# MLP of an encoder layer: weight sums on VectorE, their stores a step later, first rows and updated rows asked for steps ahead

## The chip, the cores and the metric

The kernel runs on one core of a Trainium2 chip. The metric is the device time of one execution, in microseconds (us). "Before" and "after" name the kernel without and with the change.

## The reference

One encoder layer, sequence 2048, width 1024, all in float32. Only the end of it matters here:

```python
x = x + gt1 * (mixed @ w_o)                       # end of the mixer
h = rmsnorm(x, g_norm2) * (1.0 + sc2) + sh2
x = x + gt2 * (jnp.square(jax.nn.relu(h @ w1)) @ w2)   # w1: 1024 x 4096, w2: 4096 x 1024
```

Ahead of it stand the conditioning vector, the input projection, stick-breaking attention, chunked attention and the output projection `mixed @ w_o`.

## The kernel before

Activations are kept transposed: 128 features on the partitions, 512 tokens along a row, so that there are four token blocks. A float32 product is made of three matmuls (`mm3`): ScalarE casts the operand to its high part, VectorE subtracts to get the low part (`split`), and TensorE multiplies high by high, high by low and low by high. One `operand` is thus a cast on ScalarE and a subtraction on VectorE. Operands lie in a pool of eight buffers (`opp`).

The MLP cuts its matrices into two by two quarters and makes seven products where eight would be the plain way. The operands of these products are sums and differences of quarters: quarters have the names "11", "12", "21", "22", the products the numbers 1 to 7. Product 1 uses quarter "11" itself, 2 uses "12", 4 uses "22", and 5, 6, 3 and 7 use sums that VectorE or GpSimd make (`column_sum`). The order is `OUTER = (1, 5, 6, 3, 7, 2, 4)`. Products share three banks (`HOME`): 1 and 2 the first, 5 and 3 the second, 6, 7 and 4 the third. The third bank is seeded by ScalarE with a copy of product 1 (`ps_s<-ps`); products 5 and 6 are copied out by ScalarE (`cp<-ps`) before 3 and 7 add to their banks.

The work of this last part is a list of steps, in the order in which TensorE runs them:

- `Mixed`: eight steps, one for a row block of the output projection of the last token block; 24 matmuls each. `residual` adds the result to x on VectorE, and the row is stored.
- `First(mb, j, i)`: product i of pair j (16 pairs of w1 chunks, seven products each), for the token pair `mb`, 12 matmuls. It runs for `mb` 1, and after `plain` stages for `mb` 0. A result goes through squared ReLU to the scratch `scr_hid`.
- `Second(mb, i, j)`: product i of the second matrix by hidden rows (`plain`), 16 steps of 12 matmuls. Its operands come as `hw` from `scr_hid` and w2 or `scr_s`.
- `Outer(i, q, k)`: 56 steps of 6 matmuls for one i (`outer`, for i of 7, 2, 3, 4), with a second level of seven products inside. Its operands come as `l` (weights) and `r` (hidden rows).

After the `First` steps of `mb` 1 come `plain(1, 1)`, `plain(1, 6)`, `plain(1, 5)`, then the `First` steps of `mb` 0, then `plain(0, 1)`, `outer(7)`, `plain(0, 6)`, `outer(2)`, `plain(0, 5)`, `outer(3)`, `outer(4)`.

Each engine works through its instructions in the order in which the program traces them. That order is written out by hand: `at(n, job)` puts a job at step n, and `Later.add(ticks, job)` puts one so many step ends later, with the step end of its own step counted. At each step the main loop first prepares operands of later steps as long as eight operand buffers suffice, then loads a mixer row, then makes the operands of the first two `First` steps (at the last `Mixed` step only), then traces the jobs of the step, then the step's own matmuls and what follows on them:

```python
while nxt is not None and ready - used + nxt.tiles <= 8:
    nxt.prepare()
...
for job in jobs.get(n, ()):
    job()
s.run()
...
later.tick()
```

The jobs that matter here:

- `First.load` asks for a pair of w1 chunks (two DMAs into tile `w`); `First.fetch` loads if that hasn't been done and makes the pair's four sums, in tiles `ts` (pool `tp`, seven buffers) and, for product 7, in place. For the first two pairs of `mb` 1 the sums are on GpSimd.
- `second_sums` loads w2 chunks (`w2s`) while `First` of `mb` 1 runs, makes four sums in place on VectorE and stores each to `scr_s` at once. `outer_sums` does the same with `wt` and `scr_t` while `First` of `mb` 0 runs.
- `raw_pair` gives the buffers for `w`, `w2s`, `wt`, `hw` and `l`, in turn from a ring of three and from one spare.
- `plain_loads` asks for the `hw` pairs of a `plain` stage, so many steps ahead of each.
- `load_x` asks for the rows of x (`txo` in pool `tp`, `cxo` in a pool of twelve) that an `outer` stage updates, quarter by quarter: "22" at the products 5 and 7, "12" at 6 and 3, "11" at 2, "21" at 4. `weigh` updates them on VectorE from the bank, and they are stored at the end of the step after.

All of these DMAs are issued by the one sync queue (SP), in the order of the program too: a store that waits for VectorE holds back the loads behind it.

Of the kernel before, what the change touches and what calls it, by code (L numbers as in the profile page):

```python
# [24 lines left out]
KT = D // P  # L25
# [54 lines left out]
def encoder_kernel(ctx, tc, xT, c, g1, g2, w_in, w_rest, gqk, bias, w_o, w1, w2, w_ada, b_ada, out):  # L80
# [1202 lines left out]
    PLAIN = (1, 6, 5)  # L1283
    DOUBLE = (7, 2, 3, 4)
    OUTER = (1, 5, 6, 3, 7, 2, 4)
    HOME = {1: 1, 2: 1, 5: 5, 3: 5, 6: 6, 7: 6, 4: 6}
    HP = NP // 2
    CN = TB // 2
# [5 lines left out]
    if True:  # L1294
# [138 lines left out]
        class Step:  # L1433
            tiles = frees = 1

            def prepare(self):
                pass

# [3 lines left out]
        class First(Step):  # L1442
# [4 lines left out]
            def __init__(self, mb, j, i):  # L1447
                self.mb, self.j, self.i, self.nm = mb, j, i, f"{mb}_{j}_{i}"
                if mb and j == 0 and i in OUTER[:2]:
                    self.tiles = self.frees = 0  # L1450

            def prepare(self, home=None):
                if (home is None) != (self.tiles > 0):
                    return
                d, i = First.pair[self.mb, self.j], self.i
                self.w = operand(d[{1: "11", 2: "12", 4: "22"}.get(i, i)], f"w{self.nm}", dst=home)

            def load(self):
                d, j = First.pair.setdefault((self.mb, self.j), {}), self.j
# [9 lines left out]
            def fetch(self, m=None):  # L1469
                d = self.load()  # L1470
                for n in range(4) if m is None else (m,):
                    pr, a, b, op = ((5, "21", "22", ALU.add), (6, 5, "11", ALU.subtract), (3, "12", 6, ALU.subtract), (7, "11", "21", ALU.subtract))[n]
                    d[pr] = column_sum(pool if self.mb and self.j < 2 else dve, d["21"] if pr == 7 else temp(f"s{self.nm}_{pr}"), d[a], d[b], op)
                return d

            def run(self):
# [70 lines left out]
        def second_sums(j, step):  # L1547

            t = []

            def load():
                t.append(raw_pair([P, 2, 2, TB], F32, f"w2s_{j}"))
                for s in range(2):
                    sp.dma_start(t[0][:, s].rearrange("p r n -> p (r n)"), w2[2 * j + s])

            def out(i, dst, a, b, op):
                tile = {nm: t[0][:, s, r, :] for nm, s, r in (("11", 0, 0), ("21", 0, 1), ("12", 1, 0), ("22", 1, 1))}
                column_sum(dve, tile[dst], tile[a], tile[b], op)
                sp.dma_start(scr_s[i - 1 if i < 7 else 0, j // 2][:, j % 2, :], tile[dst])

            at(step - (6 if j else 0), load)
            sums = ((5, "22", "21", "22", ALU.add), (7, "21", "11", "21", ALU.subtract))
            sums += ((6, "11", "22", "11", ALU.subtract), (3, "12", "12", "11", ALU.subtract))
            for n, x in enumerate(sums):
                at(step + n + (0 if j else 4), lambda x=x: out(*x))

        class Second(Step):

# [100 lines left out]
        def outer_sums(i, m, step):  # L1669

            t = []

            def load():
                t.append(raw_pair([P, 2, 2, TB], F32, f"wt{i}_{m}"))
                for a in range(2):
                    if i in (3, 7):
                        sp.dma_start(t[0][:, a], scr_s[i - 1 if i < 7 else 0, HP // 2 * a + m])
                        continue
                    r, s = {2: (0, 1), 4: (1, 1)}[i]
                    j = HP * a + 2 * m  # L1680
                    for q in range(2):
                        sp.dma_start(t[0][:, a, q, :], w2[2 * (j + q) + s][:, r * TB : (r + 1) * TB])

            def sums(pr, dst, a, b, op):
                v = {nm: t[0][:, h, :, c * CN : (c + 1) * CN] for nm, h, c in (("11", 0, 0), ("12", 1, 0), ("21", 0, 1), ("22", 1, 1))}
                column_sum(dve, v[dst], v[a], v[b], op)
                sp.dma_start(scr_t[i, pr][:, 2 * m : 2 * m + 2, :], v[dst])

            at(step - 6, load)
            todo = ((5, "22", "21", "22", ALU.add), (7, "21", "11", "21", ALU.subtract))  # L1690
            todo += ((6, "11", "22", "11", ALU.subtract), (3, "12", "12", "11", ALU.subtract))
            for n, x in enumerate(todo):
                at(step + n, lambda x=x: sums(*x))
# [89 lines left out]
        def outer(i, plan):  # L1783

            f = len(steps)
            steps.extend(Outer(i, q, k) for q in range(7) for k in range(HP))
            for g in range(HP // 2):
                for pr, (begin, gap) in plan["load"].items():
                    at(begin + gap * g, lambda pr=pr, g=g: half(i, pr, g))
                for pr, (begin, gap) in plan["sum"].items():  # L1790
                    at(begin + gap * g, lambda pr=pr, g=g: half_sum(i, pr, g))
            for q in range(7):
                at(f + HP * q - 12, steps[f + HP * q].load)
            for pr, b in ((5, "22"), (6, "12"), (2, "11"), (4, "21")):
                s = steps[f + HP * OUTER.index(pr)]
                at(f + HP * OUTER.index(pr) + 1, lambda s=s, b=b: s.load_x(b))
            return f

        class Mixed(Step):
# [40 lines left out]
        steps += [Mixed(0, (KT - LEFT + n) % KT, n) for n in range(KT)]  # L1840
        for n in range(KT):
            steps[n].then = lambda n=n: (
                steps[n + LEFT].load() if n + LEFT < KT else steps[KT].fetch() if n + LEFT == KT else None
            )
        for mb in (1, 0):
            begin = len(steps)
# [2 lines left out]
            for j in range(NP):  # L1849
                f = steps[begin + 7 * j]  # L1850
                if mb:
                    second_sums(j, begin + 7 * j + 2)
                else:
                    outer_sums(DOUBLE[j // 4], j % 4, begin + 7 * j + 5)
                    if j < HP:
                        for i, n in ((3, 2), (2, 5), (7, 2), (4, 5)):
                            at(begin + 7 * j + n, lambda i=i, f=f: f.other(i))
                if j > mb:
                    at(begin + max(7 * j - 13, 2 if mb else -6), f.load)
                    for m in range(4):  # L1860
                        at(begin + 7 * j - 9 + (m if j > 1 else 0), lambda f=f, m=m: f.fetch(m))
            if mb:
                for m, n in enumerate((-1, -1, 1, 2)):
                    at(begin + n, lambda m=m, f=steps[begin + 7]: f.fetch(m))
                norm2(1, begin + 18)
                norm2(0, begin + 48)
                for k in range(HK):
# [14 lines left out]
                at(f + m - (leads.pop(0) if leads else 7), steps[f + m].load)  # L1882

        f = plain(0, 1)
        plain_loads(f, [])
        e = len(steps)
        plan = {"load": {1: (f - 5, 1), 5: (f - 1, 1), 3: (f + 4, 2), 2: (f + 18, 2)}}
        plan["sum"] = {6: (f + 9, 2), 7: (f + 13, 2), 4: (f + 44, 2)}
# [50 lines left out]
        ahead = iter(steps[1:])  # L1939
        nxt = next(ahead)  # L1940
        for n, s in enumerate(steps):
            while nxt is not None and ready - used + nxt.tiles <= 8:
                nxt.prepare()
                ready += nxt.tiles
                nxt = next(ahead, None)
            for m in (0, 1) if n == 0 else (n + 1,):
                if m < KT:
                    steps[m].load_row()
            if n == KT - 1:
                firsts = spare.tile([P, 2, 2, TB], F32R, tag="r8", name="opr")  # L1950
                for m in range(2):
                    steps[KT + m].prepare(firsts[:, m])
            for job in jobs.get(n, ()):
                job()
            s.run()
            used += s.frees
            later.tick()
# [42 lines left out]
```

## Time and profile before

| | us |
|---|---|
| median of three runs | 2568.27 |
| lowest and highest | 2566.47, 2568.61 |
| the profiled execution | 2568.92 |
| its span on the page | 2567.2 |
| TensorE busy in the span | 2534.1 |
| VectorE, ScalarE, GpSimd busy | 2012.0, 1496.2, 760.8 |

How to read the lines: a row of the timeline has its start and its length in us, engine, line of the program, operation, what it writes and reads by the tiles' names, the shape, and how many instructions were merged ("x12"). A bracket gives the engine's idle time before it and who ended it. PE is TensorE, DVE VectorE, ACT ScalarE, POOL GpSimd, SPq the sync queue. Nearly all rows have line L42, which is the helper that all go through, so rows are found by tile. A row of a table of stretches gives, after the stretch, its length and the busy us (with instructions) of PE, PE's weight loads, DVE, ACT and POOL, then the granted clock of TensorE, the busy share of the DMA engines, and GB/s. A row of waits gives who waited for whom, the total, how often and the longest.

### The profile page before, as it was taken

Reading aid. Unit: us, or ns where it says so; the run is one execution under the profiler, and the core shown is the slowest. Engines: PE = TensorE matmul, PEld = TensorE weight load, DVE = VectorE, ACT = ScalarE, POOL = GpSimd, SP = SyncE. Lnnn points to the kernel's source line nnn. Section 1 sums busy time; section 2 is a strip of 40 time slices with the busy share of each in tenths; the row PEclk is TensorE's granted clock in tenths of the full one; section 3 lists DMA queues with packets and bytes.
Section 4 is the critical chain, followed back from the end, with each engine's and each line's share of the span. In section 5 each row is a group of like instructions: output and inputs, shape, how many; then the busy total and the mean of one; then the engine's idle time right before and its main releaser. Section 6 shows DMA issues by size and latency. Waiting matters only on the chain.

```text
span 2567.2 us, 39419 instructions
## 1 busy us (share of the span) xinstructions
PE 2534.1 (99%) x12436; PEld 2109.1 (82%) x12436; DVE 2012.0 (78%) x3501; ACT 1496.2 (58%) x2871; POOL 760.8 (30%) x1136
## 2 busy tenths in 40 slices
PE   9999999999999999999999999999999999999999
PEld 7888888888888888887887888888888878788887
DVE  7656767887789878998867777668978657988897
ACT  6333435668866687666755555566555545646565
POOL 4330145776776667777612000000000000000000
PEclk9999999999999999999999999999999999999999
DMA  9879978689877788756786888787899779677872
GB/s 351 332 298 363 342 281 293 213 237 290 277 239 233 238 279 272 248 193 196 224 309 243 286 285 274 260 306 267 275 323 304 273 254 409 246 272 265 291 268 82
DMA packets 293200, 698.92 MB, mean 272 GB/s; under 512 B 31360, under 2 KB 83584, under 8 KB 281856
## 3 DMA queue, kind: packets, MB, share of 16 engines
q1 hardware_dynamic: 291696, 691.69, 78.1%
q10 hardware_dynamic: 1296, 4.72, 0.5%
q8 instruction: 98, 1.61, 0.2%
q14 instruction: 110, 0.90, 0.1%
HBM read 477.66 MB, written 218.63 MB: 271 GB/s over the span
## 4 chain that ended last, share of the span: by engine, by line
PE 86%; DVE 5%; ACT 3%; DMA 2%; issue 2%; POOL 1%; SPq 1%; DVEq 0%; POOLq 0%; ACTq 0%
PE ps L42 29%; PE ps_s L42 14%; PE pt L42 11%; PE acc L42 6%; PE wt L42 6%; PE po L42 4%; PE z L42 4%; PE pf L42 4%; PE pq L42 3%; PE cz L42 2%; DVE p L42 2%; PE pso L42 1%; DVE opr L42 1%; PE ct L42 1%; ACT z L42 1%
## 5 line engine op out<-in xcount | busy, mean ns | idle before, releaser
L42 PE MATMUL ps<-h,opw 128*128 128x512 f32 x1512 | 361.7, 392 | 3.6 <-ACT cp L42 3.6
L42 ACT CAST wth<-wt 128x512 fp32r<-128x512 f32 (+3 forms) x544 | 257.4, 484 | 172.4 <-PE wt L42 162.5
L42 POOL TENSOR_TENSOR b<-p 128x512 f32<-128x512 f32 (+1 forms) x320 | 292.5, 914 | 167.9 <-DVE p L42 91.9
L42 PEld LDWEIGHTS ps<-h,opw 128*128 128x128 f32 x1512 | 285.7, 189 | 63.6 <-ACT cp L42 4.0
L42 DVE TENSOR_TENSOR wtl<-wt,wth 128x512 fp32r<-128x512 f32 (+3 forms) x544 | 291.2, 547 | 59.2 <-ACT wth L42 56.7
L42 PE MATMUL pt<-w,ht 128*128 128x512 f32 x1248 | 288.2, 391 | 0.0
L42 PE MATMUL ps_s<-h,opw 128*128 128x512 f32 x1152 | 278.6, 391 | 3.2 <-ACT ps_s L42 3.2
L42 PEld LDWEIGHTS pt<-w,ht 128*128 128x128 f32 x1248 | 233.0, 188 | 47.7
L42 PE MATMUL ps<-oph,opv 128*128 128x512 f32 x1152 | 263.8, 391 | 2.5 <-DVE txo L42 2.5
L42 DVE TENSOR_TENSOR_SCAN p<-z,p,zero 128x512 f32<-128x512 f32 x192 | 245.7, 1281 | 25.6 <-ACT z L42 18.6
L42 PEld LDWEIGHTS ps_s<-h,opw 128*128 128x128 f32 x1152 | 217.1, 189 | 48.8 <-ACT ps_s L42 3.6
L42 PEld LDWEIGHTS ps<-oph,opv 128*128 128x128 f32 x1152 | 217.2, 189 | 48.4 <-DVE txo L42 3.0
L42 PE MATMUL acc<-wth,v 128*128 128x512 f32 (+3 forms) x544 | 220.5, 409 | 0.0
L42 ACT CAST opr<-r 128x512 fp32r<-128x512 f32 x224 | 139.3, 623 | 107.7 <-PE ps L42 51.1
L42 ACT ACTIVATE z<-z 128x512 f32<-128x512 f32 (+1 forms) x320 | 166.5, 521 | 55.2 <-PE z L42 49.3
L42 PE MATMUL z<-k,q 128*128 128x512 f32 (+3 forms) x640 | 185.6, 372 | 7.7 <-DVE p L42 7.2
L42 PE MATMUL acc<-wtl,v 128*128 128x512 f32 (+3 forms) x544 | 185.4, 347 | 0.0
L42 PE MATMUL ps<-opr,ol 128*128 128x512 f32 x768 | 176.4, 389 | 0.1
L42 DVE TENSOR_TENSOR opr<-r,opr 128x512 fp32r<-128x512 f32 x224 | 151.2, 688 | 27.5 <-ACT opr L42 24.8
L42 PE MATMUL wt<-ident,b 128*128 128x128 f32 x1088 | 171.4, 273 | 1.1 <-DVE cols L42 0.3
L42 PEld LDWEIGHTS wt<-ident,b 128*128 128x128 f32 x1088 | 136.3, 140 | 42.2 <-DVE cols L42 1.8
L42 PEld LDWEIGHTS ps<-opr,ol 128*128 128x128 f32 x768 | 144.0, 188 | 30.5 <-DVE ol L42 0.4
(218 smaller groups left out, 4862.8 us busy)
## 6 DMA issues: line engine op xcount, KB each, us to landing
q<-scr_q SPq DMA_DIRECT2D x128, 256.0 KB, 4.7
w<-in_w_dram SPq DMA_DIRECT2D x64, 512.0 KB, 5.8
r<-scr_hid SPq DMA_DIRECT2D x64, 512.0 KB, 7.5
k<-scr_k SPq DMA_DIRECT2D x240, 128.0 KB, 4.3
v<-scr_v SPq DMA_DIRECT2D x120, 256.0 KB, 3.9
wa<-in_w_ada_dram SPq DMA_DIRECT2D x48, 512.0 KB, 6.4
ow<-scr_wo SPq DMA_DIRECT2D x24, 1024.0 KB, 5.8
hw<-scr_hid SPq DMA_DIRECT2D x48, 512.0 KB, 6.4
```

What stands on the lines that cost most here:

```text
L42: return lambda *x, **y: self.tc.keep_in_program_order(f(*x, **y))
```

## The change

The sums of the first two pairs move from GpSimd to VectorE. The first pair's load stays at `Mixed` step 5, but its sums are traced at the last `Mixed` step between the operands that need them; jobs of that step now come ahead of these operands. The second pair's load and sums move from the last `Mixed` step and the steps after to steps 1 to 4 of the `First` stage, and `ready()` holds back the preparing of an operand whose sum hasn't been traced. `second_sums` and `outer_sums` store each sum at the end of the next step. The first sums of `w2s` come one step earlier. The first `hw` pair of `plain(0, 1)` is asked for nine steps ahead in place of seven. The rows of the quarters "12", "11" and "21" are asked for five steps ahead of their product's first step in place of one step behind it, "22" as before.

```diff
+    OUTER_NAME = {1: "11", 2: "12", 4: "22"}
...
         class Step:
+            def ready(self):
+                return True
...
         class First(Step):
+            def ready(self):
+                return OUTER_NAME.get(self.i, self.i) in First.pair.get((self.mb, self.j), ())
...
             def fetch(self, m=None):
-                    d[pr] = column_sum(pool if self.mb and self.j < 2 else dve, d["21"] if pr == 7 else temp(f"s{self.nm}_{pr}"), d[a], d[b], op)
+                    d[pr] = column_sum(dve, d["21"] if pr == 7 else temp(f"s{self.nm}_{pr}"), d[a], d[b], op)
...
         def second_sums(j, step):
-                sp.dma_start(scr_s[i - 1 if i < 7 else 0, j // 2][:, j % 2, :], tile[dst])
+                later.add(2, lambda: sp.dma_start(scr_s[i - 1 if i < 7 else 0, j // 2][:, j % 2, :], tile[dst]))
...
-                at(step + n + (0 if j else 4), lambda x=x: out(*x))
+                at(step + n + (0 if j else 3), lambda x=x: out(*x))
...
         def outer_sums(i, m, step):
-                sp.dma_start(scr_t[i, pr][:, 2 * m : 2 * m + 2, :], v[dst])
+                later.add(2, lambda: sp.dma_start(scr_t[i, pr][:, 2 * m : 2 * m + 2, :], v[dst]))
...
         def outer(i, plan):
-                at(f + HP * OUTER.index(pr) + 1, lambda s=s, b=b: s.load_x(b))
+                at(f + HP * OUTER.index(pr) + (1 if b == "22" else -5), lambda s=s, b=b: s.load_x(b))
...
-                steps[n + LEFT].load() if n + LEFT < KT else steps[KT].fetch() if n + LEFT == KT else None
+                steps[n + LEFT].load() if n + LEFT < KT else steps[KT].load() if n + LEFT == KT else None
...
+                if j > mb or mb and j:
                     for m in range(4):
-                        at(begin + 7 * j - 9 + (m if j > 1 else 0), lambda f=f, m=m: f.fetch(m))
+                        at(begin + (m + 1 if mb and j == 1 else 7 * j - 9 + (m if j > 1 else 0)), lambda f=f, m=m: f.fetch(m))
             if mb:
-                for m, n in enumerate((-1, -1, 1, 2)):
-                    at(begin + n, lambda m=m, f=steps[begin + 7]: f.fetch(m))
...
         f = plain(0, 1)
-        plain_loads(f, [])
+        plain_loads(f, [9])
...
-            while nxt is not None and ready - used + nxt.tiles <= 8:
+            while nxt is not None and ready - used + nxt.tiles <= 8 and nxt.ready():
...
+            for job in jobs.get(n, ()):
+                job()
             if n == KT - 1:
                 firsts = spare.tile([P, 2, 2, TB], F32R, tag="r8", name="opr")
-                for m in range(2):
-                    steps[KT + m].prepare(firsts[:, m])
-            for job in jobs.get(n, ()):
-                job()
+                steps[KT].prepare(firsts[:, 0])
+                steps[KT].fetch(0)
+                steps[KT + 1].prepare(firsts[:, 1])
+                for m in range(1, 4):
+                    steps[KT].fetch(m)
             s.run()
```

More of the change, by code (lines that the diff above doesn't have):

```diff
@@ L1455, in prepare @@
                 d, i = First.pair[self.mb, self.j], self.i
-                self.w = operand(d[{1: "11", 2: "12", 4: "22"}.get(i, i)], f"w{self.nm}", dst=home)
+                self.w = operand(d[OUTER_NAME.get(i, i)], f"w{self.nm}", dst=home)
             def load(self):
```

## Prediction

> **What bounds the kernel now.** I read the page's first line and its busy shares first, then the list of what TensorE waited for, kept to the MLP (the change touches nothing ahead of it).
>
> ```profile
> span 2567.2 us, 39419 instructions
> ...
> PE 2534.1 (99%) x12436; PEld 2109.1 (82%) x12436; DVE 2012.0 (78%) x3501; ACT 1496.2 (58%) x2871; POOL 760.8 (30%) x1136
> ```
>
> ```profile
> PE ps L42 <- ACT cp L42: 3.6, 1, 3.6
> PE ps_s L42 <- ACT ps_s L42: 3.2, 1, 3.2
> PE ps L42 <- DVE txo L42: 2.5, 1, 2.5
> PE po L42 <- DMA ow<-scr_wo: 1.0, 1, 1.0
> ```
>
> TensorE is busy for 99% of the span and the change removes no matmul. All that an edit of the order can win in the MLP is therefore in three waits of TensorE, of 3.2, 3.6 and 2.5 us (the fourth line lies ahead of the MLP), and in what each wait drags behind it. I looked each up in the timeline.
>
> **First wait, start of the MLP.** TensorE rows of the first pair of w1 chunks:
>
> ```profile
> 1365.46 5.60 PE L42 MATMUL ps<-h,opr 128*128 128x512 f32 x24
> ...
> 1374.24 4.21 PE L42 MATMUL ps_s<-h,opw 128*128 128x512 f32 x12 [3.18 <-ACT ps_s L42]
> ...
> 1384.16 2.88 PE L42 MATMUL ps<-h,opw 128*128 128x512 f32 x12
> ```
>
> The price of a step comes from the chain of waits, at a place without a wait (first row), and the clock from a table of stretches (its third column from the right is the granted clock):
>
> ```profile
> 2121.12 65.28 PE ps L42 x288
> ```
>
> ```profile
> 1365.00:1390.00 25.00, 21.82 (x89) 17.59 (x88) 17.29 (x18) 11.84 (x22) 11.08 (x7) 0.93 0.39 150
> ...
> 2244.00:2260.00 16.00, 14.48 (x57) 11.81 (x58) 12.43 (x18) 4.84 (x9) 0.00 (x0) 0.89 1.03 377
> ```
>
> 65.28 us for 288 matmuls is 0.2267 us each, 2.72 us for a `First` step of 12. From 1365.46 to 1384.16 lie five steps, worth 13.60 us, and they took 18.70: 5.10 us lost, 3.2 of it standing and the rest slow. The row of 12 behind the wait lasts 4.21 us, and a mean clock of 0.93 over 25 us is 3.5 us at half rate. A wait thus costs itself and about 1.7 us more.
>
> Why it stood:
>
> ```profile
> 1360.21 0.84 SPq L42 DMA_DIRECT2D w<-in_w_dram  x2
> ...
> 1362.67 1.80 POOL L42 TENSOR_TENSOR ts<-w 128x512 f32<-128x512 f32 x1 [59.04 <-ACT h L42]
> 1363.24 0.74 DVE L42 SCALAR_TENSOR_TENSOR cxr<-pso,mod,cxr 128x512 f32<-128x512 f32 x1
> ...
> 1364.01 3.73 SPq L42 DMA_DIRECT2D scr_x<-cxr  x2
> ...
> 1369.61 2.18 ACT L42 CAST opw<-w 128x512 fp32r<-128x512 f32 x4 [1.08 <-POOL w L42]
> ...
> 1372.98 0.62 ACT L42 CAST opw<-ts 128x512 fp32r<-128x512 f32 x1 [0.67 <-POOL ts L42]
> 1373.62 0.57 ACT L42 COPY ps_s<-ps 128x512 f32<-128x512 f32 x1
> ```
>
> The third step needs the bank seeded by the copy at 1373.62. ScalarE works in order, and that copy stands behind eight casts, the last of which wait for GpSimd's sums of the *second* pair.
>
> **Second wait, end of the last `First` stage.** Here are the sync queue, ScalarE and TensorE:
>
> ```profile
> 2085.45 1.25 SPq L42 DMA_DIRECT2D scr_hid<-cz  x1
> ...
> 2091.99 4.76 SPq L42 DMA_DIRECT2D scr_t<-wt  x2
> ...
> 2099.23 0.47 SPq L42 DMA_DIRECT2D hw<-scr_hid  x1
> ...
> 2100.69 2.88 PE L42 MATMUL ps_s<-h,opw 128*128 128x512 f32 x12
> ...
> 2105.40 0.62 ACT L42 CAST oph<-hw 128x512 fp32r<-128x512 f32 x1 [6.11 <-DMA hw<-scr_hid]
> ...
> 2106.55 0.58 ACT L42 COPY cp<-ps 128x512 f32<-128x512 f32 x1
> ...
> 2107.18 5.49 PE L42 MATMUL ps<-h,opw 128*128 128x512 f32 x12 [3.61 <-ACT cp L42]
> ...
> 2118.24 2.88 PE L42 MATMUL ps_s<-h,opw 128*128 128x512 f32 x12
> ```
>
> Between 2100.69 and 2118.24 are four steps, 10.88 us, which took 17.55: 6.67 us lost. The sync queue issued nothing from 2086.7 to 2092, then two stores of `wt` that waited for VectorE's sums, and so the first `hw` load left at 2099.23 only. Its cast waited 6.11 us for it, and the copy that frees the bank stood behind the cast.
>
> **Third wait, end of the first `outer`.**
>
> ```profile
> 2222.26 2.29 SPq L42 DMA_DIRECT2D scr_x<-cxo  x4
> ...
> 2231.35 2.72 DVE L42 SCALAR_TENSOR_TENSOR cxo<-ps,mod,cxo 128x512 f32<-128x512 f32 x4
> ...
> 2234.49 4.61 SPq L42 DMA_DIRECT2D txo<-scr_x  x4
> ...
> 2241.46 1.52 PE L42 MATMUL ps<-oph,opv 128*128 128x512 f32 x6
> ...
> 2245.52 19.83 PE L42 MATMUL ps<-oph,opv 128*128 128x512 f32 x79 [2.54 <-DVE txo L42]
> ```
>
> ```profile
> 2311.36 10.88 PE ps_s L42 x48
> ```
>
> From 2241.46 to 2311.36 are again 288 matmuls (16 `Second` steps of 12 and 16 `Outer` steps of 6), which cost 69.90 instead of 65.28 us: 4.62 lost. The rows `txo` of quarter "21" were asked for at 2234.49, behind stores that waited for VectorE's `cxo`, and came after the bank was done.
>
> In all 5.10 + 6.67 + 4.62 = 16.4 us.
>
> The Trainium skill, "TensorE: Matmul & The Clock Gate", section "What's actually happening", has the clock halved after about one idle window of 3.4 us, in windows that run free of the kernel. By that rule only the 3.61 us wait would drag a slow stretch, and the three would be worth 3.2 + 6.7 + 2.5 = 12.4 us. This trace differs: 2.54 us of standing was enough (0.89 over 16 us is 3.5 us at half rate). The measurement decides.
>
> **The change part by part.**
>
> ```profile
> L42 DVE TENSOR_TENSOR ts<-w x30: 681/685/694, 1385.6 to 2072.9; 128x512 f32<-128x512 f32 x30
> ...
> DMA to landing us min/median/max: 4.2/5.7/7.4
> ```
>
> ```profile
> w2s<-in_w_dram SPq DMA_DIRECT2D x2, 512.0 KB, 3.6
> ```
>
> (The first is the durations of the sums, the second the landing times of all w1 chunks, the third that of two loads issued at 1371.13 into an idle queue.)
>
> *Sums on VectorE, in the new order.* Eight sums go from GpSimd to VectorE at 0.69 us. VectorE is in order: last row but one of the mixer till 1363.98, low part of "11" 1364.67, sum 5 1365.36, then ScalarE's cast (0.62) 1365.98, low part of 5 1366.67, sums 6, 3 and 7 at 1367.36, 1368.05, 1368.74, the last mixer row 1369.5. TensorE's second step begins at 1368.18, so its operand is in time. ScalarE casts 6, 3, 7, "12", "22" behind the sums, till 1370.6, and the copy ends at 1371.2. `ready()` keeps the second pair's casts behind it. Due is 1365.46 + 5.44 = 1370.90, so 0.3 us late.
>
> The second pair's load moves from 1360.21 to step 9, on the sync queue behind the store of the last mixer row, about 1369.8. Its first sum stands on VectorE in front of the first pair's combinations, and two of its casts on ScalarE in front of the copy of product 6, which TensorE needs for the first pair's fifth step at 1376.3. Landing 3.6 to 5.7 us after the second issue (1370.2): 1373.8 to 1375.9; sum, cast and copy add 1.9, so 1375.7 to 1377.8: a new wait of 0 to 1.5 us. The slowest landing of the trace, 7.4, makes it 3.2, plus the slow clock 5.0. I take 0.3, because the load then goes into an idle queue, as the 3.6 us row did. First part: 5.1 - 0.6 = 4.5 us won, bounds 0 to 5.1.
>
> *Stores a step later, first `hw` nine steps ahead.* The `hw` load comes two steps earlier in the order, and the `wt` sums' stores no longer stand between. The queue is free at 2086.7; the buffer that it takes is an older chunk's, already consumed. With the 6.1 us of the row it lands by 2093, and its cast, due about 2099, waits for nothing. A late store keeps a `wt` or `w2s` buffer a step longer; the next load into it comes some 14 steps after the previous one, and an earlier store would have waited on the same sum. I cost that at nothing; without that cover it is 2.7 us on one load. Won: 6.67 us, bounds 0 to 6.7.
>
> *Rows six steps ahead.* An `Outer` step of 6 is 1.36 us, so three of four quarters are asked for 8.2 us earlier; "21" then takes the place of 2224.6, right behind the stores of 2222.26, 9.9 us before its old issue. It was 2.5 us late. `tp` has seven buffers, and quarters "12" and "21" of this stage take eight; the "12" stores are issued long before, so none waits. The rows' 1 MB goes in front of an `l` load, which has 12 steps, 16 us, of lead. Won: 4.6 us, bounds 0 to 4.6.
>
> Sum: 4.5 + 6.7 + 4.6 = 15.8 us. The profiled execution took 2568.92 us (its span and 1.7 around it), 0.65 above the median of the three runs. So 2553.1 by that execution, and 2552.5 as the median.
>
> **The rivals.**
>
> *The wait moves to the second pair.* That is the 3.2 us case above with its slow clock: little of the first part is left, 2557. For it speaks that the load leaves 9 us later than before; against it, the idle queue.
>
> *The transfers are the next thing late.*
>
> ```profile
> 2090.00:2095.00 5.00, 5.00 (x23) 4.13 (x23) 1.95 (x3) 2.86 (x5) 0.00 (x0) 1.00 0.15 52
> ...
> 2120.00:2125.00 5.00, 5.00 (x23) 4.14 (x23) 2.18 (x4) 4.02 (x8) 0.00 (x0) 1.00 1.05 406
> ```
>
> ```profile
> 2149.76 0.62 ACT L42 CAST oph<-hw 128x512 fp32r<-128x512 f32 x1 [4.28 <-DMA hw<-scr_hid]
> ```
>
> At 2120 the 16 engines are full. The thirteenth `hw` operand is cast at 2149.76, ready some 1.9 us later, and used at 2121.12 + 12 x 2.72 = 2153.8: 2 us of room. TensorE now comes 6.7 us earlier; if the loads don't, 4.7 us of wait plus 1.7 of clock give the second part back: 2559. Against it: the loads start earlier too, into a stretch that moved only 52 GB/s.
>
> *Slower: the early rows block the sync queue.* If in the four `outer` stages a row's buffer is free only when it used to be asked for, the queue stands up to 8.2 us with `l`, `r` and `hw` loads behind it. Each of 12 such places would cost about 2.5 us with the clock: 30 us, 2568.3 - 15.8 + 30 = 2582; from seven places on the kernel is slower. Against it: the eight-of-seven count above is the tightest, and there the buffers are free.
>
> *It does not reach the waits.* If the casts stay where they were in the order, nothing changes: 2568.
>
> **How the numbers follow.** About 0.2% (5.1 us) can be told from no change. Forecast 0.62 (2550.5 to 2555); moved wait 0.13 (2557); transfers 0.13 (2559); blocked queue 0.07 (2582); not reached 0.05 (2568). The first three are faster: 0.88; same 0.05; slower 0.07. The range goes from 2550.5 (nothing new late, and half a microsecond of small waits gone) to 2560, which takes in the second and third case.
>
> **What would show it.** Right: no TensorE wait over 1 us in the MLP, no clock below 1 there, the copy `ps_s` at about 1371, the first `hw` load before 2092, `txo` of "21" landed before its bank's end, no GpSimd sums. Wrong: a wait of TensorE for `cp` near 1376, casts waiting for `hw` with TensorE standing between 2130 and 2150, or sync-queue waits on `txo` stores ahead of `l` loads.

## The result, and the profile after

| | before | after |
|---|---|---|
| median of five runs on one chip, us | 2568.61 | 2556.26 |
| lowest and highest | 2566.47, 2569.26 | 2554.80, 2558.06 |
| the profiled execution | 2568.92 | 2554.99 |

The ratio is 0.9951, with a 95% interval from 0.9941 to 0.9962: the change wins 12.4 us, where the forecast was 15.8. The median of 2556.26 lies above the band that the prediction called its forecast (2550.5 to 2555) and inside its whole range (up to 2560). The two profiled executions differ by 13.9 us, since the one of after lies 1.3 below its median. Two further sets of runs gave 0.9954 and 0.9956 (below).

The page after, its first line and its busy shares:

```profile
span 2553.3 us, 39361 instructions
...
PE 2528.9 (99%) x12436; PEld 2104.6 (82%) x12436; DVE 2010.0 (79%) x3509; ACT 1496.9 (59%) x2871; POOL 747.7 (29%) x1128
```

The work is the same: as many matmuls, eight sums more on VectorE and eight fewer on GpSimd. The list of TensorE's waits in the MLP (total, how often, longest):

```profile
PE ps L42 <- ACT opv L42: 0.6, 2, 0.4
PE ps_s L42 <- ACT cp L42: 0.3, 1, 0.3
PE ps_s L42 <- DVE opr L42: 0.3, 1, 0.3
```

The waits of 3.2, 3.6 and 2.5 us are gone. In their places stand a wait for `cp` of 0.3 and two for `opv`, an operand made from `hw`, of 0.6 together. The wait for `opr` lies in a later `outer` stage and was there before, about as long.

The start of the MLP in the timeline of after:

```profile
1364.74 5.60 PE L42 MATMUL ps<-h,opr 128*128 128x512 f32 x24
...
1369.04 0.88 SPq L42 DMA_DIRECT2D w<-in_w_dram  x2
1369.71 0.57 ACT L42 COPY ps_s<-ps 128x512 f32<-128x512 f32 x1
1370.33 3.02 PE L42 MATMUL ps_s<-h,opw 128*128 128x512 f32 x12
...
1374.53 0.69 DVE L42 TENSOR_TENSOR ts<-w 128x512 f32<-128x512 f32 x1 [2.92 <-DMA w<-in_w_dram]
...
1375.78 0.58 ACT L42 COPY cp<-ps_s 128x512 f32<-128x512 f32 x1
1376.41 3.06 PE L42 MATMUL ps_s<-h,opw 128*128 128x512 f32 x12 [0.34 <-ACT cp L42]
1379.31 2.89 PE L42 MATMUL ps<-h,opw 128*128 128x512 f32 x12
```

The copy that seeds the third bank ends at 1370.28, and the third step follows at 1370.33. The second pair's load leaves at 1369.04; its sum holds VectorE for 2.92 us, and the copy of product 6 comes 0.34 us late. Five steps take 1379.31 - 1364.74 = 14.57 us, 0.97 above their 13.60; before it was 5.10.

The end of the last `First` stage:

```profile
2081.96 0.50 SPq L42 DMA_DIRECT2D hw<-scr_hid  x1
...
2094.26 0.61 ACT L42 CAST oph<-hw 128x512 fp32r<-128x512 f32 x1
...
2095.97 0.59 ACT L42 COPY cp<-ps 128x512 f32<-128x512 f32 x1 [0.57 <-PE ps L42]
...
2098.49 2.88 PE L42 MATMUL ps<-h,opw 128*128 128x512 f32 x12
```

The first `hw` load leaves 17.3 us earlier, while TensorE is 4.9 earlier at the start of this stage; its cast has no bracket, and the copy behind the cast now waits for TensorE instead of the other way round. The end of the first `outer`:

```profile
2214.83 1.88 SPq L42 DMA_DIRECT2D txo<-scr_x  x4
...
2231.80 2.72 DVE L42 SCALAR_TENSOR_TENSOR txo<-ps_s,mod,txo 128x512 f32<-128x512 f32 x4
```

The rows of quarter "21" are asked for 17 us ahead of their update, which starts as soon as the bank is done. What is new stands between, in `plain(0, 1)`:

```profile
2135.72 0.62 ACT L42 CAST oph<-hw 128x512 fp32r<-128x512 f32 x1 [7.08 <-DMA hw<-scr_hid]
2136.99 6.01 PE L42 MATMUL ps<-oph,opv 128*128 128x512 f32 x24 [0.26 <-ACT opv L42]
...
2142.15 0.62 ACT L42 CAST oph<-hw 128x512 fp32r<-128x512 f32 x1 [4.17 <-DMA hw<-scr_hid]
...
2143.35 11.51 PE L42 MATMUL ps<-oph,opv 128*128 128x512 f32 x48 [0.36 <-ACT opv L42]
```

Before, ScalarE waited for `hw` three times in this stage, 3.2, 4.6 and 4.3 us, and TensorE never stood. Now the three waits are 4.8, 7.1 and 4.2 us, and TensorE stands twice.

The next table has the time of each stage, from its first matmul to the first of the next, taken from the timelines of all profiled executions. The upper line is what the matmuls alone take at the prices of the prediction (2.72 us for 12, 1.36 for 6).

| profiled kernel | `First`, mb 1 | `First`, mb 0 | `plain(0, 1)` | `outer(7)` | `plain(0, 6)` |
|---|---|---|---|---|---|
| matmuls alone | | 304.64 | 43.52 | 76.16 | 43.52 |
| before | 313.54 | 311.31 | 43.52 | 76.98 | 47.98 |
| after | 309.43 | 304.64 | 45.33 | 76.99 | 43.85 |
| after_again | 309.01 | 304.64 | 45.80 | 76.99 | 43.86 |
| after_third | 308.85 | 304.64 | 46.33 | 76.98 | 43.87 |
| sums_alone | 309.03 | 311.11 | 43.52 | 76.99 | 47.89 |
| lead_alone | 314.95 | 307.81 | 44.14 | 76.99 | 45.89 |
| stores_alone | 311.63 | 304.64 | 48.84 | 77.01 | 47.69 |
| rows_alone | 311.75 | 314.43 | 43.52 | 76.99 | 43.85 |
| second_early | 309.20 | 304.64 | 46.17 | 76.99 | 43.87 |
| r_later | 309.83 | 304.64 | 43.52 | 80.37 | 43.87 |
| both_fixes | 309.58 | 304.64 | 43.52 | 80.41 | 43.86 |
| behind2 | 313.03 | 304.64 | 46.34 | 76.98 | 43.85 |
| behind4 | 314.59 | 304.64 | 46.19 | 76.99 | 43.85 |
| r_some_later | 310.19 | 304.64 | 48.08 | 78.66 | 43.87 |

Each row is one execution. From before to after: -4.1, -6.7, +1.8, 0, -4.1 us, in all -13.1. The other 0.8 lie mostly ahead of the MLP, whose start varies by 2.0 us over these profiles, so they are not the change's. The three `plain` stages of mb 1, not shown, vary from 130.6 to 132.4, which the change does not touch either.

### The profile page after: what moved, and what is told of

It reads as the page before. It is cut to its first block, busy times and chain, and to the rows that moved or that the text cites. A ratio compares the mean times of both kernels' runs of the same rounds, so it can differ in the third digit from the quotient of the medians.

```text
span 2553.3 us, 39361 instructions
## 1 busy us (share of the span) xinstructions
PE 2528.9 (99%) x12436; PEld 2104.6 (82%) x12436; DVE 2010.0 (79%) x3509; ACT 1496.9 (59%) x2871; POOL 747.7 (29%) x1128
```

## The experiments

The theory: each of the first three waits has its own edit, as the prediction says, and what the result lacks against it is mostly the transfers of `plain(0, 1)`. The rivals: two of the edits are needed together for one wait or one of them is idle; what is left is a late second pair at the MLP's start; the sums' place on VectorE costs time elsewhere. The diffs of lead_alone, stores_alone and rows_alone are against before, all others against after.

### The parts one by one

These four were compared with before on one chip (before's median there 2568.85).

**sums_alone**: the sums on VectorE in their new order; the stores, the lead and the rows as before.

```diff
-                later.add(2, lambda: sp.dma_start(scr_s[...], tile[dst]))
+                sp.dma_start(scr_s[...], tile[dst])
...
-                later.add(2, lambda: sp.dma_start(scr_t[...], v[dst]))
+                sp.dma_start(scr_t[...], v[dst])
...
-                at(f + HP * OUTER.index(pr) + (1 if b == "22" else -5), lambda s=s, b=b: s.load_x(b))
+                at(f + HP * OUTER.index(pr) + 1, lambda s=s, b=b: s.load_x(b))
...
-        plain_loads(f, [9])
+        plain_loads(f, [])
```

> Only the first part (sums of the first two pairs on VectorE, new order at the last mixer step, second pair's load in the first stage); stores, hw lead and rows as before. Theory (each part takes away its own wait, and they add): the first wait of 3.2 us goes, 0.3 us is left at the fifth First step, the waits of 3.6 and 2.5 us stay with their slow clock: about 4.1 us under the kernel before. Rival (the sync queue had to be freed as well): the 3.2 us wait stays or comes back at the second pair, under 2 us won.

Measured: 2566.79 us, ratio 0.9991 (0.9982 to 1.0001). Its timeline, TensorE rows that waited:

```profile
1377.32 3.04 PE L42 MATMUL ps_s<-h,opw 128*128 128x512 f32 x12 [0.17 <-ACT cp L42]
...
2105.51 4.50 PE L42 MATMUL ps<-h,opw 128*128 128x512 f32 x12 [4.08 <-ACT cp L42]
...
2242.64 7.58 PE L42 MATMUL ps<-oph,opv 128*128 128x512 f32 x25 [2.45 <-DVE txo L42]
```

The first wait is gone and the other two stay. Its stage gains 4.5 us in the profile; the whole gains 2.3 by the ratio, with an interval from 4.6 gained to 0.3 lost, which holds 4.5 but does not confirm it. The edit moves the sums to VectorE and also puts the second pair's load, sums and casts behind the copy that seeds the bank, and no run separates the two. An estimate from the rows before: with GpSimd's sums kept and only the second pair's casts put behind the copy, ScalarE would have cast the first pair's last operands by about 1371.3 and ended the copy at about 1371.9, 1.0 us after it was due; it ended at 1374.19, 3.3 after. So most of this wait would go by the order alone.

**lead_alone**: only the first `hw` pair nine steps ahead, the rest as before.

```diff
         f = plain(0, 1)
-        plain_loads(f, [])
+        plain_loads(f, [9])
```

> Only the first hw pair of plain(0, 1) is asked for nine steps ahead in place of seven; the wt stores stay immediate. Theory: in the sync queue the load then stands behind one wt store only (issued at 2092 before), so it leaves at about 2092.5, lands by 2098.7 and the 3.6 us wait goes: about 6.7 us won less what the transfers of plain(0, 1) take back (1.8 us in the changed kernel), so 5. Rival (the stores held it up, the lead alone does not help): the load still leaves after 2097 and less than 3 us is won.

Measured: 2562.76 us, ratio 0.9980 (0.9971 to 0.9989). From its timeline:

```profile
1943.66 3.01 PE L42 MATMUL ps_s<-h,opw 128*128 128x512 f32 x12 [1.17 <-DVE cp L42]
...
2097.70 0.46 SPq L42 DMA_DIRECT2D hw<-scr_hid  x1
...
2104.47 0.61 ACT L42 CAST oph<-hw 128x512 fp32r<-128x512 f32 x1
```

The cast has no bracket: the second wait is gone with two steps of lead alone. The load leaves at 2097.70 and not at the expected 2092.5; counted from the start of `First` of mb 0, that is 3.6 us earlier than before. But the stage still takes 307.81 us, in place of 304.64, most of it for waits of 1.17, 0.92 and 0.18 for VectorE. (This execution took 2566.10 us, 3.3 above its median, so not every execution need have them.) What holds VectorE up shows in the lists of waits for the stretch from 1800 to 2105, here lead_alone:

```profile
SPq L42 <- DVE wt L42: 94.9, 40, 4.9
...
DVE ts L42 <- DMA scr_hid<-to: 24.9, 7, 4.9
```

and after:

```profile
DVE ts L42 <- DMA scr_hid<-to: 14.4, 7, 2.8
...
SPq L42 <- DVE ca L42: 52.8, 15, 4.9
SPq L42 <- DMA scr_t<-wt: 46.1, 19, 6.1
...
SPq L42 <- DVE wt L42: 0.3, 1, 0.3
```

With stores issued at once the sync queue stands 94.9 us in this stretch for sums of `wt`; result rows `to` leave later behind it, and a `ts` buffer comes free later. But before, whose queue stands just as long for these sums (99.8 us by the same list), has none of these small waits. And with late stores the queue does not stand less: it waits for other results (`ca`, 52.8 us) and, ahead of the next load into a `wt` buffer, for the late stores to land (46.1 us). So this chain is argued and not shown, and what the small waits take stays open.

**stores_alone**: both stores a step later and the first `w2s` sums a step earlier, the rest as before.

```diff
-                sp.dma_start(scr_s[...], tile[dst])
+                later.add(2, lambda: sp.dma_start(scr_s[...], tile[dst]))
...
-                at(step + n + (0 if j else 4), lambda x=x: out(*x))
+                at(step + n + (0 if j else 3), lambda x=x: out(*x))
...
-                sp.dma_start(scr_t[...], v[dst])
+                later.add(2, lambda: sp.dma_start(scr_t[...], v[dst]))
```

> Only the stores of the w2s and wt sums a step later (and the first w2s sums a step earlier); hw lead, rows and First sums as before. Theory (either of the two edits would do): with the stores of the last two sums behind it the hw load leaves at about 2092.5 and the 3.6 us wait goes: 5 us won. Rival (only the lead matters): load after 2097, wait stays, under 2 us either way.

Measured: 2565.16 us, ratio 0.9981 (0.9970 to 0.9993). From its timeline:

```profile
2091.35 0.41 SPq L42 DMA_DIRECT2D hw<-scr_hid  x1
...
2098.07 0.61 ACT L42 CAST oph<-hw 128x512 fp32r<-128x512 f32 x1
...
2141.39 6.03 PE L42 MATMUL ps<-oph,opv 128*128 128x512 f32 x24 [0.85 <-ACT opv L42]
...
2149.04 13.14 PE L42 MATMUL ps<-oph,opv 128*128 128x512 f32 x48 [1.62 <-ACT opv L42]
```

The second wait is gone here too, and entirely: the stage takes 304.64. Either edit removes it, so lead and stores do not add there. What the lead adds is seen in `plain(0, 1)`, if the other two edits of the change, which act elsewhere, leave that stage alone: without the lead it takes 48.84 us, 5.3 over its matmuls, in two waits of 0.85 and 1.62 us for `hw` operands and one stretch at half clock behind the second. That is the prediction's second rival at nearly its price of 6.4. With the lead (after) 1.8 to 2.8 of it remain.

**rows_alone**: only the rows asked for six steps earlier.

```diff
-                at(f + HP * OUTER.index(pr) + 1, lambda s=s, b=b: s.load_x(b))
+                at(f + HP * OUTER.index(pr) + (1 if b == "22" else -5), lambda s=s, b=b: s.load_x(b))
```

> Only the rows of quarters 12, 11 and 21 six steps earlier. Theory: the 2.5 us wait of the first outer stage goes with its slow clock, 4.6 us won; the other two waits stay. Rival (rows in front of operand loads, or buffers short): new waits of DVE or TensorE for l, r or hw in the outer stages, less than 2 us won or slower.

Measured: 2566.33 us, ratio 0.9992 (0.9982 to 1.0001). From its timeline:

```profile
2110.56 4.62 PE L42 MATMUL ps<-h,opw 128*128 128x512 f32 x12 [4.11 <-ACT cp L42]
...
2243.79 2.72 DVE L42 SCALAR_TENSOR_TENSOR txo<-ps_s,mod,txo 128x512 f32<-128x512 f32 x4
```

The third wait is gone, the second stays, and no new wait of TensorE for an `l`, `r` or `hw` operand appears: `plain(0, 6)` has the 43.85 us of after. The total gains 2.0 us by the ratio, not the 4.6 expected. In the profiled execution `First` of mb 0, which the edit does not touch, took 314.43 us with small waits of the kind that lead_alone has; whether the other executions lose their time there is not shown.

By the ratios the parts gain 2.3, 5.1 or 4.9 (lead or stores) and 2.0 us, each to within 2.3 to 3.1. That is 9 us in all against 11 to 13 for the whole, which agrees within the noise and shows no more; that the parts add is read from the table by stages.

### What is left

Compared with before on a second chip (before's median 2569.63), in five rounds.

**after_again**: the changed kernel once more.

> The changed kernel itself, as the reference on the same chip for the three beside it: 2555 to 2558, TensorE waits of 0.3 us near 1376, 2137 and 2143.

Measured: 2556.49 us, ratio 0.9954 (0.9941 to 0.9966); `plain(0, 1)` takes 45.80 us. Of the three waits of 0.3 us that were expected, this execution has none of that size: TensorE waits once, at 2144.70, for 1.13 us.

**second_early**: the second pair's load before the `First` stage, its sums kept.

```diff
             if j > mb or mb and j:
+                if mb and j == 1:
+                    at(begin - 1, f.load)
                 for m in range(4):
```

> The changed kernel with the second pair's chunks asked for at the last mixer step again (their sums stay where they are). Theory (the late load is what is left of the first wait): cast of the second pair no longer waits for a DMA, the 0.34 us wait at the fifth First step goes, 0.5 to 0.8 us won. Rival (ScalarE and VectorE alone make it late): wait stays.

Measured: 2556.78 us, ratio 0.9952 (0.9940 to 0.9965), the same as after_again. The start of the MLP in its timeline:

```profile
1372.04 3.06 PE L42 MATMUL ps_s<-h,opw 128*128 128x512 f32 x12 [0.42 <-ACT ps_s L42]
```

The wait of 0.34 us at the fifth step is gone, and one of 0.42 at the third has come in its place. Its timeline shows why: with the chunks already there, ScalarE makes four casts of `w` (2.19 us) ahead of the copy that seeds the bank, in place of three (1.67). The stage stays within the three values of after, and the 0.5 to 0.8 us expected did not come: an earlier load of the second pair, placed so, is not what the result lacks.

**r_later**: the first `outer` stage's hidden rows asked for later, so that they are not in front of the late `hw` loads, and their sums later with them. All four sums for product 7 of this stage then take one of their two terms from the rows of the next stage, so this kernel and both_fixes do not compute the layer; they are read here for where the time goes alone.

```diff
-        plan = {"load": {1: (f - 5, 1), 5: (f - 1, 1), 3: (f + 4, 2), 2: (f + 18, 2)}}
-        plan["sum"] = {6: (f + 9, 2), 7: (f + 13, 2), 4: (f + 44, 2)}
+        plan = {"load": {1: (f + 3, 2), 5: (f + 8, 2), 3: (f + 13, 2), 2: (f + 20, 2)}}
+        plan["sum"] = {6: (f + 20, 2), 7: (f + 28, 2), 4: (f + 44, 2)}
```

> The changed kernel with the hidden rows r for the first outer stage (1, 5, 3, 2) asked for 8, 9, 9 and 2 steps later, and two of their sums later, so that 4 MB leave the crowded stretch of plain(0, 1). Theory (the transfers are what takes back 1.8 us there, and what makes the times of the changed kernel spread over 3 us): the cast's waits for hw of 5 to 7 us and the TensorE waits of 0.26 and 0.36 us near 2137 and 2143 go, about 1.8 us won, all runs within 1 us. Rival (the loads are late because of buffers or the order of the queue, not bandwidth): waits for hw stay. Second rival: r comes late for the outer stage, a new wait of TensorE or DVE for r after 2150.

Measured: 2557.93 us, ratio 0.9957 (0.9943 to 0.9971). ScalarE's wait for `hw` from 2080 to 2160, after and then r_later (total, how often, longest):

```profile
ACT oph L42 <- DMA hw<-scr_hid: 16.3, 4, 7.1
```

```profile
ACT oph L42 <- DMA hw<-scr_hid: 10.3, 4, 4.1
```

With less in front of them the `hw` loads come in time, TensorE waits for none, and `plain(0, 1)` is back at its 43.52 us. That confirms the transfers in their stage. The load of the thirteenth operand takes as long to land as in after (6.4 us); it is issued 21.2 us after the stage's start instead of 26.3, so what it gains is its place in the queue. The executions still spread over 2.5 us, though 1 was expected, so the spread has another reason. In `outer(7)` more is lost than was won, 80.37 in place of 76.99. A table of stretches shows why (length, then busy us of PE, PE's loads, DVE, ACT and POOL; granted clock; DMA share; GB/s), r_later and then after:

```profile
2170.00:2180.00 10.00, 10.00 (x46) 8.26 (x44) 10.00 (x15) 6.19 (x12) 0.00 (x0) 1.00 1.03 419
2180.00:2190.00 10.00, 9.59 (x40) 7.00 (x39) 10.00 (x16) 5.86 (x11) 0.00 (x0) 1.00 0.85 335
```

```profile
2170.00:2180.00 10.00, 10.00 (x46) 8.29 (x45) 8.81 (x15) 6.41 (x12) 0.00 (x0) 1.00 1.02 412
2180.00:2190.00 10.00, 10.00 (x46) 8.29 (x45) 9.24 (x15) 6.46 (x12) 0.00 (x0) 1.00 0.47 166
```

VectorE was at 8.8 to 9.2 of 10 us already; with the moved sums it is full, and TensorE's 46 matmuls of 10 us fall to 40. All of TensorE's listed waits in this stage are for `opr`, an operand that VectorE makes.

**both_fixes**: the edits of second_early and of r_later together.

> The changed kernel with both edits (second pair early, r later). Theory: they add, 2.3 to 2.6 us under the changed kernel, near 2553.5, no TensorE wait over 0.3 us in the MLP. Rival: no more than the better one alone.

Measured: 2559.37 us, ratio 0.9961 (0.9948 to 0.9974). A miss: the two edits were expected to add up to 2.3 to 2.6 us. By the stages above, second_early has nothing to add and r_later's gain is lost again in `outer(7)` (80.41).

### How late the second pair may come

Compared with before on a third chip (before's median 2569.26). **behind2** and **behind4**: two or four loads of 256 KB that nothing uses are issued ahead of the second pair's load.

```diff
             if j > mb or mb and j:
+                if mb and j == 1:
+                    def unused():
+                        for n in range(2):          # behind4: 4
+                            sp.dma_start(kept(f"unused{n}"), xT[n * P : (n + 1) * P, 0:TB])
+
+                    at(begin + 1, unused)
                 for m in range(4):
```

> The changed kernel with two unused loads of 256 KB in the sync queue ahead of the second pair's chunks. It prices a wait of middle length. Landing about 1.3 us later: the 0.34 us wait at the fifth First step becomes about 1.6 us. If the clock drops after any wait (as it did after 2.5, 3.2 and 3.6 us), 1.3 + 1.7 = 3 us slower than the changed kernel; if it drops only after longer ones, 1.3 us slower with the clock at 1.

> The same with four unused loads, 1 MB. Landing about 2.6 us later: a wait of about 2.9 us at the fifth First step, the case of the prediction's first rival. With the slow clock 2.6 + 1.7 = 4.3 us slower than the changed kernel; by a rule that only a whole idle window of 3.4 us halves the clock, 2.6 us slower.

Measured: 2562.23 us, ratio 0.9972 (0.9961 to 0.9983), and 2564.00, ratio 0.9977 (0.9968 to 0.9987). The fifth step of behind2, then of behind4:

```profile
1379.53 4.61 PE L42 MATMUL ps_s<-h,opw 128*128 128x512 f32 x12 [2.21 <-ACT cp L42]
```

```profile
1380.02 4.33 PE L42 MATMUL ps_s<-h,opw 128*128 128x512 f32 x12 [4.15 <-ACT cp L42]
```

The wait of the prediction's first rival appears at the place that it named, and `First` of mb 1 takes 3.8 and 5.4 us more than about 309.2 without the loads: the wait, and 1.6 and 1.2 us of half clock behind it. Both waits are longer than the 1.6 and 2.9 us expected, so the cover of this load is thinner than I took it for. In the changed kernel it is just used up: the load overruns it by 0.34 us in the profile of after.

### The hidden rows at another place

Compared with before once more (before's median 2569.61), in five rounds. **after_third**: the changed kernel.

> The changed kernel again, as the reference beside the next run: 2555 to 2558, plain(0, 1) at 45.3 to 46.2 us against 43.5 for its matmuls.

Measured: 2558.86 us, ratio 0.9956 (0.9943 to 0.9968). The two waits of `plain(0, 1)` in its timeline:

```profile
2140.06 6.02 PE L42 MATMUL ps<-oph,opv 128*128 128x512 f32 x24 [0.52 <-ACT opv L42]
...
2147.22 11.45 PE L42 MATMUL ps<-oph,opv 128*128 128x512 f32 x48 [1.14 <-ACT opv L42]
```

Together they are 1.7 us, where after had 0.6: the same program loses 1.8, 2.3 and 2.8 us in this stage in its three profiles. Both the time and the stage (46.33) came out just above what was expected.

**r_some_later**: the rows moved by fewer steps, the first sums by two.

```diff
-        plan = {"load": {1: (f - 5, 1), 5: (f - 1, 1), 3: (f + 4, 2), 2: (f + 18, 2)}}
-        plan["sum"] = {6: (f + 9, 2), 7: (f + 13, 2), 4: (f + 44, 2)}
+        plan = {"load": {1: (f + 1, 2), 5: (f + 2, 2), 3: (f + 5, 2), 2: (f + 18, 2)}}
+        plan["sum"] = {6: (f + 11, 2), 7: (f + 13, 2), 4: (f + 44, 2)}
```

> The changed kernel with fewer transfers moved than in r_later and with the sums left nearly where they were: rows r of 1 from six steps later and every other step, of 5 three steps later and every other step, of 3 one step later, one sum two steps later; 2 MB leave the stretch ahead of the late hw loads. Theory (bandwidth ahead of the hw loads is what takes back 2 us; in r_later VectorE's moved sums, not the transfers, cost 3.4 us in the outer stage): plain(0, 1) at 43.5 to 44, outer(7) at 77, 1.8 to 2.5 us under the changed kernel. Rival (the rows r are needed where they were): outer(7) again over 79 us, nothing won.

Measured: 2562.12 us, ratio 0.9966 (0.9954 to 0.9978). A miss, worse than after in both stages. From its timeline:

```profile
2146.05 0.62 ACT L42 CAST oph<-hw 128x512 fp32r<-128x512 f32 x1 [6.86 <-DMA hw<-scr_hid]
...
2147.27 13.00 PE L42 MATMUL ps<-oph,opv 128*128 128x512 f32 x48 [2.44 <-ACT opv L42]
```

The rows moved out of the earlier stretch and into the one of the last `hw` loads, which come later than in after. The load of the thirteenth operand lands 33.9 us after the stage's start, against 32.7 in after and 27.6 in r_later. It agrees with the cause (what is in front of the late `hw` loads) and refutes the size that I gave it. Whether some place for the rows spares both `plain(0, 1)` and `outer(7)` stays open. No kernel here beat the changed one.

## Why the prediction was right, point by point

**First wait**, 4.5 us forecast, 4.1 measured. Counted from TensorE's first row, the copy that seeds the bank was worked out to end at 5.7 us, due at 5.4; it ended at 1370.28 - 1364.74 = 5.5. The new wait at the fifth step, costed at 0.3, is 0.34. The five steps lose 0.97 and not 0.6; in the two further profiles of this kernel they lose 0.52 and 0.36, which makes 0.6 in the mean. What the wait cost without the edit varies more: 5.10 us in before, 6.51, 3.19 and 3.31 in lead_alone, stores_alone and rows_alone, whose code is the same at this place. So 4.1 is one pair of executions, and the means give 3.9.

The small value of the new wait was in part luck. It rested on a landing time of 3.6 us in an idle queue. The first of the two loads landed after 3.67 us, the second, which the sum needs, after 5.03, with two loads of `w2s` issued 0.9 us behind it. By the prediction's own sum that is 0.8 us late, and TensorE, itself late by then, stood for 0.34. behind2 and behind4 show what a later one costs.

**Second wait**, 6.67 forecast, 6.67 measured; `First` of mb 0 takes exactly its 112 steps. The working named two reasons together (the lead, and no `wt` stores between); the runs show that either one removes this wait. The prediction put the later freeing of `wt` buffers at nothing. TensorE did lose nothing by it, but the sync queue stood 46.1 us in this stage behind late stores that had yet to land, up to 6.1 us for one load, so there was less cover than the working said. What the pair buys is elsewhere: none of the ten profiles with late stores has the small waits of lead_alone and rows_alone in this stage (before and sums_alone, with stores at once, have none of their size either), and with the lead `plain(0, 1)` does not lose the 5.3 us of stores_alone.

**Third wait**, 4.6 forecast, 4.1 measured. Of the 4.62 counted, 4.46 lay in `plain(0, 6)` (47.98 against 43.52); 0.33 of it stays (43.85). rows_alone has the same 43.85 with no other edit.

**The step that failed** is the transfers, set aside with "the loads start earlier too, into a stretch that moved only 52 GB/s". That is so for the first `hw` load only. It leaves 17.3 us earlier, the second 10.7, and the late ones less, because they stand in a queue behind full engines: by the list of the queue's waits from 2095 to 2152 in after, it stood 8.1 us for rows `r` and 7.3 for older `hw` loads to land, and 1.0 for the operand that frees a buffer. By the two timelines the load of the thirteenth operand is issued at 2135.68 instead of 2143.16, 7.5 us earlier, while TensorE starts the stage at 2109.37 instead of 2120.96, 11.6 earlier. So 4.1 us of room were lost where the prediction had counted 2.0: some 2.1 late, and 1.8 to 2.8 (mean 2.3) were lost in the stage. That is the sign that the prediction had named for being wrong (casts waiting for `hw` with TensorE standing between 2130 and 2150), and in the two further profiles one wait there is over 1 us (1.13 and 1.14). The prediction had the 2 us of room and the 6.7 by which TensorE gains on these loads, and then dropped the case for a reason that fits another load. It came at about a third of its price of 6.4, because the late loads did move, only by less than TensorE.

By stages, 4.1 + 6.7 + 4.1 - 2.3 = 12.6 us, against 12.4 by the medians of the first set and 11.8 and 11.3 by the ratios of the other two. The forecast of 2552.5 is 3.8 us below the median of after, and the transfers' 2.3, the first wait's 0.4 and the third's 0.5 make most of it. The range held because it took in this case, to which the prediction gave 0.13.

**The rivals.** The moved wait did not come, apart from the 0.34 us; made to come, it costs what was said, wait and slow clock. The sync queue is not blocked by the early rows: rows_alone shows no new wait of TensorE in the `outer` stages. The casts did move: not reached is out.

**The clock.** The prediction took 1.7 us of half clock behind each wait of before, against the rule of the Trainium skill, "TensorE: Matmul & The Clock Gate", section "What's actually happening", that an idle window of about 3.4 us is needed. The rows bear it out that less than such a window can do: 48 matmuls took 13.14 us behind a wait of 1.62 (stores_alone) and 11.51 behind one of 0.36 (after), 1.6 more. But it does not come behind each wait of this size. The first wait was followed by no half clock in stores_alone and rows_alone (2.20 us each), nor the third in lead_alone (2.08), so the 1.7 us in the price of a wait are not certain; the last section shows on what they depend.

## What to carry to other kernels

When a stall goes, move every later event by the time won and ask which loads move with it: those issued into an idle queue keep their lead, while those that stand behind a full stretch of transfers move only as far as the transfers ahead of them, and there a few us of room can be the next thing late. A cheap copy that frees a bank is as late as the slowest load whose cast stands ahead of it on the same in-order engine, so either give that load lead or let nothing that waits stand ahead of it on its queue; here either was enough. A fix that moves work into a stage where another engine is about nine tenths busy can give the time back there.

## What the hardware showed that was not expected

**The clock falls after waits much shorter than its slow stretch.** All stretches at half rate in the MLP last 3.41 us, or twice that (behind the waits of 3.45 and 3.61 us). One followed waits of 1.62, 2.21, 2.44, 2.45 and 4.15 us, among others; none followed one of 2.20 in stores_alone and in rows_alone or of 2.08 in lead_alone:

```profile
1373.52 3.03 PE L42 MATMUL ps_s<-h,opw 128*128 128x512 f32 x12 [2.20 <-ACT ps_s L42]
```

```profile
2244.30 5.96 PE L42 MATMUL ps<-oph,opv 128*128 128x512 f32 x25 [2.08 <-DVE txo L42]
```

The first takes 3.03 us for 12, where behind2's, after a wait of 2.21, takes 4.61. So the length alone does not decide; where the wait lies does. In every trace with more than one such stretch, their starts are whole multiples of 3.413 us apart: in before they start at 1375.79, 2106.24 and 2246.19, which is 214.0 and 41.0 steps. The windows that run free of the kernel in the Trainium skill, "TensorE: Matmul & The Clock Gate", section "What's actually happening", agree with that; the need for a whole idle window does not.

Cut into these windows, the time that TensorE stood within one window tells the cases apart. Of the 13 windows of the MLP, over all profiles, in which it stood for 1.70 us or more at full rate, 12 were followed at once by half rate; the other one, 1.91 us in sums_alone, was not. None was that held 1.67 us or less. The wait of 2.20 in stores_alone fell on two windows (0.86 and 1.35 us), the one of 2.21 in behind2 into one. So it took about half a window of standing here, and whether a wait of 2 us costs 1.7 us more depends on where it falls.

**VectorE is slower beside GpSimd's sums.** VectorE's subtractions in the timeline before, while GpSimd made sums, and after:

```profile
1363.90 1.12 DVE L42 TENSOR_TENSOR opr<-w,opr 128x512 fp32r<-128x512 f32 x1
...
1365.16 1.56 DVE L42 TENSOR_TENSOR opr<-ts,opr 128x512 fp32r<-128x512 f32 x1
```

```profile
1363.35 0.68 DVE L42 TENSOR_TENSOR opr<-w,opr 128x512 fp32r<-128x512 f32 x1
...
1365.32 0.69 DVE L42 TENSOR_TENSOR opr<-ts,opr 128x512 fp32r<-128x512 f32 x1 [0.69 <-ACT opr L42]
```

The same instructions took 1.6 and 2.3 times as long. Both ended 0.55 us after the sum that GpSimd was making when they began (1364.47 and 1366.17), and so did the next six subtractions of VectorE, as if the input had to wait for that sum to end. The row updates `cxr` in between, which read a bank, took the same 0.74 us with GpSimd running and without. The Trainium skill, "GPSIMD Engine Reference", section "1. Specifications", has the two engines share their interfaces to SBUF, with contention when an instruction of VectorE has two inputs there, which agrees. Sums that GpSimd took off VectorE thus cost VectorE time all the same: about 0.4 to 1.1 us for each of its eight subtractions that met one, against 0.69 us for the sum itself. The prediction's first part had that in its favour without counting it.
